# A decoder layer's down projection: token sums stored by gate and up, operands streamed eight tiles ahead, no GpSimd work

## The chip, the core and the metric

The kernel runs on one core of one Trainium2 chip. The metric is device time in microseconds (us); the median of three runs of the kernel before is 1282.82 us (1282.78 to 1285.71). The engines have short names below: PE is TensorE, DVE is VectorE, ACT is ScalarE, POOL is GpSimd, and SP is SyncE, which issues every DMA of this kernel.

## The reference

The layer normalises its input, projects it, runs differential attention and gated linear attention, projects back, and adds the residual; all of this is unchanged. What the change touches is the feed-forward part, for 1024 tokens, a model width of 1024 and 2816 hidden features:

```python
m = rms_norm(h, ffn_norm_gain[l])
h = h + (jax.nn.silu(m @ w_ffn_gate[l]) * (m @ w_ffn_up[l])) @ w_ffn_down[l]
```

`rms_norm` multiplies each token by one factor, 1/sqrt(mean of squares + eps), and each feature by a gain. Everything is float32.

## The kernel before, in words

**Matrix products.** Tensors lie transposed, features on partitions and tokens along the free dimension. A float32 product is made of three fp32r products: each operand is split into a high half (an ACT copy, L248) and a low half (a DVE subtraction, L249) by `split`, and `mm3` (L256 to L259) issues high x high, high x low and low x high, each 128x128 by 128x512.

**Strassen's scheme.** Gate, up and down each multiply two-by-two block matrices in seven products (Winograd's form) in place of eight. The operands are sums and differences of blocks, and the results are sums of the seven products, some of which are accumulated in the same PSUM banks.

**Gate and up** (L1042 to L1107) run over 11 pairs `pr` of feature blocks, each pair for the gate matrix (m = 0) and the up matrix (m = 1). In a pair, `both` runs the seven products with the operands B11, B21, T1, T2, B22, T3 and T4 of the normalised tokens; `a_operands` makes the weight operands a, b, c, d, e, f and g in order, two matrices each, in a ring of four slots (`uh`, `ul`). The sums among them are made by POOL, and by DVE in pair 0. `result` reads a finished quarter q (two token halves by two feature blocks): for the gate it multiplies by the token factor `rsh` and runs the silu on ACT; for up it multiplies with the gate's result into `ac`. Where an earlier partial result has to be added first, the up side's multiplication is POOL's (L1072; DVE's in pair 0). At the end of a pair one DMA of 1 MB stores `ac` in DRAM. The up side's token factor is put off: it is linear, so it is applied at the end of down, to the projected result.

**Pair 0** also makes the token operands T1 to T4 on ACT and DVE (`b_operands`) and the token factor (`rstd_half`).

**Down** (L1115 to L1257) has seven products too, in the order 1, 2, 7, 6, 5, 3, 4, each over 11 steps j and four PSUM banks k, so 12 matmuls a step. Operand a is a sum of activation blocks, operand b one of weight blocks. `sums` loads a raw tile when it needs one and keeps A for later sums; POOL makes the sums of a, DVE those of b. `cut` splits both in rings of three slots. `multiply` issues a product; what stands in `beside` is issued between its steps: reads of finished banks, the token factor, the residual and the stores. In products 5, 3 and 4 POOL's order is the written one. Down's first operands are loaded while the last pair still runs.

**Order.** Except where `manual_schedule` names an engine, a scheduler orders each engine's instructions by its own model of their times; with it, the named engine follows the text. Each engine executes its instructions in order, and a waiting instruction holds up what is behind it on that engine. That holds for SP's queue of DMAs as well: a DMA whose target or source isn't ready holds up the DMAs behind it.

**Memory.** A tile pool that is closed gives its SBUF to the pools opened after it, and a new tile waits for those whose place it takes. `ntp` holds the split tokens, `fl` T2 to T4 and small tiles, `bp` the tiles `gt` and `ac` in two slots each.

Of the kernel before, what the change touches and what calls it, by code (L numbers as in the profile page):

```python
# [9 lines left out]
F32 = mybir.dt.float32  # L10
# [8 lines left out]
P = 128  # L19
T = 1024  # L20
# [136 lines left out]
def decoder_layer(ctx: ExitStack, tc, xt, vecs, lams, w_proj, w_up, w_gu, w_dn, out):  # L157
# [115 lines left out]
    wctx, actx = ExitStack(), ExitStack()  # L273
    wp = wctx.enter_context(pool("wp"))
# [612 lines left out]
    def rstd_half(hf):  # L887
        ps = psum.tile([P, 512], F32, name=f"hn{hf}", tag="ms")
        nc.tensor.matmul(ps, ones, sums[hf], start=True, stop=True)
        a, u = (fl.tile([P, 512], F32, name=f"{nm}{hf}", tag="u2", bufs=2) for nm in "au")  # L890
# [76 lines left out]
    fl = fctx.enter_context(pool("fl"))  # L967
    act_d = [dram.tile([P, 2, T], F32, name=f"act{pr}") for pr in range(NJ // 2)]
# [37 lines left out]
    def a_operands(pr, m):  # L1006
# [11 lines left out]
        def sub(op, a, b, nm):  # L1018
            r = fl.tile([P, 4, P], F32, name=f"{nm}f{pr}_{m}", tag="sf", bufs=4)
# [22 lines left out]
    for pr in range(NJ // 2):  # L1042
# [8 lines left out]
        ac = bp.tile([P, 2, T], F32, name=f"ac{pr}", tag=f"B{pr % 2}")  # L1051
        quarter = lambda q: ac[:, q // 2, 512 * (q % 2) : 512 * (q % 2) + 512]

        def snap(ps, nm, m):
            r = fl.tile([P, 512], F32, name=f"{nm}{pr}_{m}", tag=nm, bufs=2)
            nc.scalar.copy(r, ps)
            return r

        def result(m, q, ps, add):

            if m == 0:
                rs = rsh[:, 512 * (q % 2) : 512 * (q % 2) + 512]
# [53 lines left out]
    with pool("dw") as dw, pool("de") as de, pool("dl") as dlp:  # L1116
        A = {q: [(de if q == "11" else dlp).tile([P, 512], F32, name=f"A{q}_{j}") for j in range(NB)]
             for q in ("11", "12", "21", "22")}
        B = {q: [dlp.tile([P, 512], F32, name=f"B{q}_{j}") for j in range(NB)] for q in ("12", "22")}

        def load_a(q, j):
            t, jj = int(q[0]) - 1, NB * (int(q[1]) - 1) + j
            nc.sync.dma_start(A[q][j], act_d[jj // 2][:, jj % 2, 512 * t : 512 * t + 512])
            return A[q][j]

        def load_b(q, j):
            dst = B[q][j] if q in B else dw.tile([P, 512], F32, name=f"Bs{q}_{j}", tag="bs", bufs=3)
            nc.sync.dma_start(dst, w_dn[int(q[1]) - 1, NB * (int(q[0]) - 1) + j])
            return dst

        def cut(src, nm, tag):
            h = dw.tile([P, 512], F32R, name=f"{nm}h", tag=f"{tag}h", bufs=3)
            l = dw.tile([P, 512], F32R, name=f"{nm}l", tag=f"{tag}l", bufs=3)
            split(src, h, l)
            return h, l

        def temp(nm, tag):
            return dw.tile([P, 512], F32, name=nm, tag=tag, bufs=2)

        def sums(i, j):  # L1140

            asub, aadd = nc.gpsimd.tensor_sub, nc.gpsimd.tensor_add
            bsub, badd = nc.vector.tensor_sub, nc.vector.tensor_add
            if i == 1:
                return load_a("11", j), load_b("11", j)
            if i == 2:
                return load_a("12", j), load_b("21", j)
            if i == 7:
                a = load_a("21", j)
                asub(a, A["11"][j], a)  # L1150
                b, c = load_b("12", j), load_b("22", j)
                bsub(b, c, b)
                return a, b
            if i == 6:
                a = A["21"][j]
                asub(a, load_a("22", j), a)
                b = B["12"][j]
                badd(b, b, load_b("11", j))
                return a, b
            if i == 5:  # L1160
# [16 lines left out]
        def multiply(i, ps, first, beside=(), then=None):  # L1177
# [3 lines left out]
            ab = []  # L1181
            for j in range(NB):
                a, b = sums(i, j)
                ab.append((cut(a, f"da{i}_{j}", "ca"), cut(b, f"db{i}_{j}", "cb")))
                if then is None or j < NB - 2:
                    for k in range(4):
                        one(i, j, k, ps, first, *ab[j])
# [14 lines left out]
        def load_h(q, k):  # L1202
            hr = dw.tile([P, 512], F32, name=f"hr{q}_{k}", tag="hr", bufs=3)
# [3 lines left out]
        def store(q, k, r):  # L1207
# [4 lines left out]
        def tokens(q):  # L1212
            return rsh[:, 512 * (int(q[0]) - 1) : 512 * (int(q[0]) - 1) + 512]

        def last(q, k, ps, r):

            add_last(q, k, scale_last(q, k, ps), r)

        def scale_last(q, k, ps):
            t = dw.tile([P, 512], F32, name=f"t{q}_{k}", tag="st", bufs=4)  # L1220
            nc.vector.tensor_mul(t, ps, tokens(q))
            return t

        def add_last(q, k, t, r):
            nc.vector.tensor_add(r, r, t)
            store(q, k, r)

        def prepare(q, k, r):

            h = load_h(q, k)  # L1230
            nc.gpsimd.tensor_mul(r, r, tokens(q))
            nc.gpsimd.tensor_add(r, r, h)
# [6 lines left out]
        U = banks("U", ("mm", "ms"))  # L1239
        multiply(1, U, True)  # L1240
        for k in K:
            nc.scalar.copy(p1[k], U[k])
        multiply(2, U, False)
        V = banks("V", ("s", "tr"))
        multiply(7, V, True, [lambda k=k: last("11", k, U[k], load_h("11", k)) for k in K])
        for k in K:
            nc.scalar.copy(p7[k], V[k])
        multiply(6, V, False, [lambda k=k: nc.gpsimd.tensor_sub(p7[k], p1[k], p7[k]) for k in K])
        W = banks("W", ("mm", "ms"))
        with tc.manual_schedule(engines=POOL):  # L1250
            multiply(5, W, True, [lambda k=k: both(k) for k in K] + [lambda k=k: prepare("22", k, c22[k]) for k in K])
            t22 = [scale_last("22", k, W[k]) for k in K]
            multiply(3, W, False, [lambda k=k: add_last("22", k, t22[k], c22[k]) for k in K]
                     + [lambda k=k: prepare("12", k, p7[k]) for k in K])
            multiply(4, V, False, [lambda k=k: last("12", k, W[k], p7[k]) for k in K]
                     + [lambda k=k: prepare("21", k, p1[k]) for k in K],
                     lambda k: last("21", k, V[k], p1[k]))  # L1257
# [53 lines left out]
```

## Time and profile before

| | |
|---|---|
| Runs, us | 1285.71, 1282.78, 1282.82; median 1282.82 |
| Profiled execution, us | 1281.03, with a span of 1279.2 from the first instruction to the last |
| Busy in the span | PE 1215.4 us (95%), DVE 849.6 (66%), ACT 578.9 (45%), POOL 381.5 (30%) |
| Mean granted clock of PE | 0.989 |
| DMA | 109.86 MB, 86 GB/s over the span |

The shares are means over stages that differ: attention, the output projection, pair 0 of gate and up until about 635 us, pairs 1 to 10 until 1027.95, then down. Below, "busy" is the time in which an engine worked on an instruction; matmuls are pipelined, so PE's busy time counts a matmul's whole passage, and the pitch from start to start is the better measure. The granted clock is given as a share of the full 2.4 GHz. A wait is idle time of an engine ahead of an instruction, put down to what came last of the things it waited for. The chain of waits goes back from the last instruction, at each step to what released it.

### The profile page before, as it was taken

How to read it: one execution, taken by the hardware profiler on the slowest of the kernel's cores; microseconds unless marked ns; L12 is line 12 of the kernel's file. 1: busy time of each engine (PE TensorE's matmuls, PEld its weight loads, DVE VectorE, ACT ScalarE, POOL GpSimd, SP SyncE). 2: the span in 40 equal slices, each digit the busy share in tenths (PEclk: the TensorE clock that was granted, in tenths of full speed). 3: DMA queues.
4: the chain of work that ended last, by engine and by line, in shares of the span. 5: the costliest groups of instructions: out<-in, count | busy, mean ns of one | idle time of the engine just before them, and what ended most of it. 6: DMA issues, size and time to landing. Idle time of an engine off the chain costs nothing.

```text
span 1279.2 us, 17033 instructions
## 1 busy us (share of the span) xinstructions
PE 1215.4 (95%) x6068; PEld 1010.8 (79%) x6068; DVE 849.6 (66%) x1722; ACT 578.9 (45%) x1171; POOL 381.5 (30%) x354
## 2 busy tenths in 40 slices
PE   7899998999889999999899999999999999898888
PEld 7789888889788887887688888888888887677666
DVE  6764588754888677539754554444555447978987
ACT  5656353665445575526433333333333434343322
POOL 4501314002340000000133543334434204535690
PEclk9999999999999999999999999999999999999999
DMA  6101010201101712410211222121222299610213
GB/s 207 44 22 58 1 50 17 68 16 51 50 17 59 206 58 84 140 67 25 98 66 38 95 99 99 66 72 61 99 99 79 70 314 324 215 60 18 66 50 107
DMA packets 54487, 109.86 MB, mean 86 GB/s; under 512 B 5617, under 2 KB 25218, under 8 KB 50178
## 3 DMA queue, kind: packets, MB, share of 16 engines
q1 hardware_dynamic: 54402, 108.77, 25.3%
q8 instruction: 48, 0.79, 0.3%
q14 instruction: 37, 0.30, 0.1%
HBM read 85.16 MB, written 23.59 MB: 85 GB/s over the span
## 4 chain that ended last, share of the span: by engine, by line
PE 72%; DVE 16%; issue 3%; ACT 3%; POOL 3%; DMA 3%; SPq 0%; DVEq 0%; POOLq 0%; ACTq 0%
PE X L259 6%; PE X L257 6%; PE X L258 6%; PE pp L257 5%; PE pp L259 5%; PE pp L258 4%; PE s L406 3%; PE Z L258 3%; PE Z L259 3%; PE Z L257 3%; PE po L450 2%; PE po L257 2%; PE po L259 2%; PE po L258 2%; PE pa L645 2%
## 5 line engine op out<-in xcount | busy, mean ns | idle before, releaser
L257 PE MATMUL pp<-wh,nh 128*128 128x384 f32 (+1 forms) x512 | 184.5, 361 | 9.9 <-ACT wh L253 7.0
L259 PE MATMUL pp<-wh,nl 128*128 128x384 f32 (+1 forms) x512 | 176.6, 346 | 0.3 <-DVE nl L249 0.3
L258 PE MATMUL pp<-wl,nh 128*128 128x384 f32 (+1 forms) x512 | 176.5, 345 | 0.4 <-DVE wl L254 0.4
L257 PEld LDWEIGHTS pp<-wh,nh 128*128 128x128 f32 x512 | 97.9, 191 | 19.5 <-ACT wh L253 7.4
L1021 POOL TENSOR_TENSOR S1f<-fr 128x512 f32<-128x512 f32 x20 | 31.7, 1587 | 257.9 <-DMA fr<-in_w_gu 257.9
L259 PEld LDWEIGHTS pp<-wh,nl 128*128 128x128 f32 x512 | 97.1, 190 | 3.2 <-issue 2.4
L258 PEld LDWEIGHTS pp<-wl,nh 128*128 128x128 f32 x512 | 97.7, 191 | 2.5 <-DVE wl L254 1.5
L1072 POOL TENSOR_TENSOR ac<-ac,gt 128x512 f32<-128x512 f32 x30 | 45.7, 1524 | 162.8 <-DVE ac L1071 158.1
L419 ACT ACTIVATE e<-e,nm 128x128 f32<-128x128 f32 (+7 forms) x64 | 49.3, 771 | 32.9 <-DVE nm L411 32.8
L546 POOL TENSOR_TENSOR go<-go,gs 128x1024 f32<-128x1024 f32 x4 | 10.2, 2538 | 142.6 <-ACT gs L545 142.6
L257 PE MATMUL po<-mh,wh 128*128 128x512 f32 x128 | 51.2, 401 | 0.0
L259 PE MATMUL po<-mh,wl 128*128 128x512 f32 x128 | 50.6, 395 | 0.0
L258 PE MATMUL po<-ml,wh 128*128 128x512 f32 x128 | 50.4, 394 | 0.0
L1067 ACT ACTIVATE gt<-gt 128x512 f32<-128x512 f32 x44 | 27.7, 632 | 46.7 <-DVE gt L1066 46.6
L254 DVE SCALAR_TENSOR_TENSOR wl<-wr,vec,wh 128x384 fp32r<-128x384 f32 (+1 forms) x64 | 39.3, 640 | 11.6 <-ACT wh L253 11.5
L621 POOL TENSOR_TENSOR X<-bT 128x64 f32<-128x64 f32 x48 | 18.8, 391 | 86.4 <-ACT bT L590 68.6
L249 DVE TENSOR_TENSOR uel<-S4f,ueh 128x512 fp32r<-128x512 f32 x22 | 18.3, 831 | 37.6 <-ACT ueh L248 37.6
L249 DVE TENSOR_TENSOR ufl<-S3f,ufh 128x512 fp32r<-128x512 f32 x22 | 15.1, 692 | 42.1 <-ACT ufh L248 42.1
L411 DVE CUSTOM_DVE_ANT_0 e<-s,ndist 128x512 f32<-128x512 f32 (+3 forms) x64 | 36.8, 586 | 8.1 <-PE s L406 6.5
L450 PE MATMUL po<-v,wT 128*128 128x128 f32 x288 | 39.9, 284 | 2.0 <-ACT wT L440 2.0
L253 ACT ACTIVATE wh<-wr,vec 128x384 fp32r<-128x384 f32 (+1 forms) x64 | 37.4, 613 | 9.0 <-DMA wr<-in_w_proj 6.3
L1021 POOL TENSOR_TENSOR S4f<-fr,S2f 128x512 f32<-128x512 f32 x20 | 29.3, 1467 | 40.4 <-DVE ucl L249 25.5
(598 smaller groups left out, 3646.5 us busy)
## 6 DMA issues: line engine op xcount, KB each, us to landing
fr<-in_w_gu SPq DMA_DIRECT2D x22, 1024.0 KB, 4.9
wr<-in_w_proj SPq DMA_DIRECT2D x72, 192.0 KB, 2.4
act<-ac SPq DMA_DIRECT2D x11, 1024.0 KB, 3.9
A<-act SPq DMA_DIRECT2D x44, 256.0 KB, 5.2
Bs<-in_w_dn SPq DMA_DIRECT2D x44, 256.0 KB, 3.6
B<-in_w_dn SPq DMA_DIRECT2D x22, 256.0 KB, 5.2
h<-in_xt SPq DMA_DIRECT2D x16, 256.0 KB, 5.0
hd<-h SPq DMA_DIRECT2D x16, 256.0 KB, 2.0
```

Of the source, the lines that this page charges most:

```text
L249: nc.vector.tensor_sub(lo, raw, hi.bitcast(F32))
L253: nc.scalar.activation(hi, src, AF.Copy, scale=gain)
L254: nc.vector.scalar_tensor_tensor(lo, src, gain, hi.bitcast(F32), ALU.mult, ALU.subtract)
L257: nc.tensor.matmul(ps, ah, bh, start=first, stop=False, **k)
L258: nc.tensor.matmul(ps, ah, bl, start=False, stop=False, **k)
L259: nc.tensor.matmul(ps, al, bh, start=False, stop=last, **k)
L406: nc.tensor.matmul(ps[m][:, :n], self.qk["q", hq][a][r, P * iq : P * iq + P], self.qk["k", ch][b][r, :n], start=(j == 0), stop=(j == 2))
L411: nc.vector.tensor_tensor_reduce(e[m][:, 512 * ch : 512 * ch + n], ps[m][:, :n], ndist[:, o : o + n], scale=-slope, scalar=nm[:, m, 0:1] i ...
L419: nc.scalar.activation(e[m][:, :cols], e[m][:, :cols], AF.Exp, bias=nm[:, m, nch - 1 : nch], scale=-1.0, accum_out=l[:, m : m + 1])
L450: nc.tensor.matmul(po[:, 0:P], self.wT[i, g][:, P * k : P * k + P], self.v[g][:, k, :], start=(kb == 0), stop=(kb == i))
L1021: (eng.tensor_sub if op == "-" else eng.tensor_add)(r, a, b)
L1072: (nc.vector if pr == 0 else nc.gpsimd).tensor_mul(quarter(q), quarter(q), gt[:, q, :])
```

## The change

- In gate and up, the gate's silu is multiplied by the token factor once more, so that what is stored is complete and down has no token factor left.
- At each pair's end DVE makes four sums of the pair's quarters (`token_sums`): quarter 1 is overwritten by q0 - q1, and `sm` takes q3 less the new quarter 1, that plus q0, and q2 less the first of them. Seven tiles are stored, in two DMAs (`keep`), where there were four. For this, the two feature blocks of a pair are now the two halves of the inner dimension.
- In the last pair, from T3 on, the compute engines follow the written order: the pair's last products, the splitting of down's steps 0 to 2 between them, then the rest of the results, the sums and the store.
- In down, operand a is loaded ready-made, 77 tiles, 8 steps ahead (`load_step`). All weight tiles are loaded once and kept; DVE makes their sums, in place where it can. Operands are cut 3 steps ahead, in rings of five slots. All compute engines follow the written order, and POOL has nothing to do.
- p1, p7 and c22 are read bank by bank at the end of products 1, 7 and 5 (`then`), the last two steps being ordered by bank for it. The residual is added by DVE.
- Tile pools move: `fl` keeps only T2 to T4 and closes with the tokens, the rest goes to `fq`; a spacer `edge` of 24 elements is added.

```diff
+EDGE = 24
+COMPUTE = {mybir.EngineType.PE, mybir.EngineType.Activation, mybir.EngineType.DVE, mybir.EngineType.Pool}
...
+    fl = ntctx.enter_context(pool("fl"))
+    fq = fctx.enter_context(pool("fq", 1, "right"))
+    act_d = [dram.tile([P, 7, 512], F32, name=f"act{pr}") for pr in range(NJ // 2)]
+    A_OF = {1: 0, 7: 1, 2: 2, 4: 3, 6: 4, 5: 5, 3: 6}
...
+        def read(m, q, ps, add):
+
+            dst = gt[:, q, :] if m == 0 else quarter(q)
+            if add is not None:
+                nc.vector.tensor_add(dst, ps, add)
+            elif m == 0:
+                nc.vector.tensor_mul(dst, ps, tokens(q))
+            else:
+                nc.vector.tensor_mul(dst, gt[:, q, :], ps)
+
+        def rest(m, q, add):
+
+            g = gt[:, q, :]
+            if m == 0:
+                if add is not None:
+                    nc.vector.tensor_mul(g, g, tokens(q))
+                nc.scalar.activation(g, g, AF.Silu)
+                nc.vector.tensor_mul(g, g, tokens(q))
+            elif add is not None:
+                (nc.vector if pr == 0 else nc.gpsimd).tensor_mul(quarter(q), quarter(q), g)
+
         def result(m, q, ps, add):
...
+            read(m, q, ps, add)
+            rest(m, q, add)
+
+        def token_sums(sm, k):
+            if k == 0:
+                nc.vector.tensor_sub(quarter(1), quarter(0), quarter(1))
+                nc.vector.tensor_sub(sm[:, 0, :], quarter(3), quarter(1))
+                nc.vector.tensor_add(sm[:, 1, :], sm[:, 0, :], quarter(0))
             else:
...
+                nc.vector.tensor_sub(sm[:, 2, :], quarter(2), sm[:, 0, :])
+
+        def keep(sm):
+            nc.sync.dma_start(act_d[pr][:, 0:4, :], ac)
+            nc.sync.dma_start(act_d[pr][:, 4:7, :], sm)
...
-        both(X, "T3", False, lambda m: result(m, 3, X[m], p5[m]))
-        both(X, "T4", False, lambda m: result(m, 2, X[m], None))
-        nc.sync.dma_start(act_d[pr], ac)
-    fctx.close()
+        if pr + 1 < NJ // 2:
+            both(X, "T3", False, lambda m: result(m, 3, X[m], p5[m]))
+            both(X, "T4", False, lambda m: result(m, 2, X[m], None))
+            token_sums(sm, 0)
+            token_sums(sm, 1)
+            keep(sm)
+
+    cuts = [[next(ops[m]) for m in range(2)] for _ in range(2)]
+    tail = ExitStack()
+    tail.enter_context(tc.manual_schedule(engines=COMPUTE))
+    for m in range(2):
+        product(X[m], cuts[0][m], bop["T3"], False)
+        read(m, 3, X[m], p5[m])
+    for m in range(2):
+        product(X[m], cuts[1][m], bop["T4"], False)
     ntctx.close()
...
+        ORDER = (1, 2, 7, 6, 5, 3, 4)
+        steps = [(i, j) for i in ORDER for j in range(NB)]
+
+        CUT, LOAD = 3, 8
+        b_left = [("21", j) for j in range(NB)] + [(q, j) for j in range(NB) for q in ("22", "12")]
...
+        def load_step(n):
+
+            if n >= len(steps):
+                return
+            i, j = steps[n]
+            araw[n] = da.tile([P, 512], F32, name=f"A{i}_{j}", tag="ar", bufs=LOAD + 2)
+            nc.sync.dma_start(araw[n], act_d[j][:, A_OF[i], :])
+            if i == 1:
+                load_b("11", j)
+            for _ in range(0 if n < LOAD else 1 + (n % 2 if n > 14 else 0)):
+                if b_left:
+                    load_b(*b_left.pop(0))
...
+        def operand_b(i, j):
+            sub, add = nc.vector.tensor_sub, nc.vector.tensor_add
+            b = {q: B[q][j] for q in B}
             if i == 7:
...
+                sub(b["12"], b["22"], b["12"])
+            elif i == 6:
+                add(b["12"], b["12"], b["11"])
+            elif i in (5, 4):
+                t = dw.tile([P, 512], F32, name=f"T{i}_{j}", tag="sb", bufs=3)
+                sub(t, b["22"] if i == 5 else b["21"], b["12"])
+                return t
+            return b[{1: "11", 2: "21", 7: "12", 6: "12", 3: "22"}[i]]
+
+        def cut_step(n):
+            if n < len(steps):
+                i, j = steps[n]
+                ab[i, j] = cut(araw.pop(n), f"da{i}_{j}", "ca"), cut(operand_b(i, j), f"db{i}_{j}", "cb")
...
             for j in range(NB):
...
+                load_step(n0 + j + LOAD)
+                cut_step(n0 + j + CUT)
...
+        for n in range(LOAD):
+            load_step(n)
+        cut_step(0)
+        cut_step(1)
+        rest(0, 3, p5[0])
+        rest(1, 3, p5[1])
+        read(0, 2, X[0], None)
+        cut_step(2)
+        rest(0, 2, None)
+        token_sums(sm, 0)
+        read(1, 2, X[1], None)
+        token_sums(sm, 1)
+        keep(sm)
+        fctx.close()
...
+        U = banks("U", ("ms", "s"))
+        multiply(1, U, True, then=lambda k: nc.scalar.copy(p1[k], U[k]))
         multiply(2, U, False)
...
+        V = banks("V", ("mm", "tr"))
+        multiply(7, V, True, [lambda k=k: last("11", k, load_h("11", k), U[k]) for k in K],
+                 lambda k: nc.scalar.copy(p7[k], V[k]))
+        multiply(6, V, False, [lambda k=k: nc.vector.tensor_sub(p7[k], p1[k], p7[k]) for k in K])
+        W = banks("W", ("ms", "s"))
+        multiply(5, W, True, [lambda k=k: both(k) for k in K],
+                 lambda k: nc.vector.tensor_add(c22[k], c22[k], W[k]))
+        multiply(3, W, False, [lambda k=k: last("22", k, c22[k], load_h("22", k)) for k in K]
+                 + [lambda k=k: (residual("12", k, p7[k]), residual("21", k, p1[k])) for k in K])
+        multiply(4, V, False, [lambda k=k: last("12", k, p7[k], W[k]) for k in K],
+                 lambda k: last("21", k, p1[k], V[k]))
```

## Rows read from the trace of the kernel before

**Rows 1.** Stretches of gate and up: us, each engine busy (instructions), granted clock, DMA share, GB/s.

```profile
640.00:1027.95 387.95, 387.95 (x1664) 311.64 (x1663) 196.03 (x253) 142.20 (x243) 157.01 (x107) 1.00 0.22 81
...
591.00:640.00 49.00, 43.46 (x173) 32.74 (x172) 42.07 (x69) 25.64 (x46) 4.46 (x4) 0.97 0.18 65
```

**Rows 2.** Stretches of down by product: the second, third, fifth and sixth, and the whole.

```profile
1058.12:1090.77 32.65, 30.54 (x134) 24.62 (x132) 23.68 (x30) 13.08 (x25) 13.48 (x9) 1.00 0.97 336
1090.77:1129.94 39.17, 32.99 (x134) 23.91 (x132) 38.80 (x46) 14.08 (x25) 22.21 (x14) 1.00 0.60 189
...
1161.84:1201.82 39.98, 34.44 (x133) 26.19 (x132) 39.91 (x40) 13.83 (x23) 30.04 (x19) 0.91 0.14 40
1201.82:1239.96 38.14, 33.37 (x132) 25.67 (x133) 34.34 (x28) 12.44 (x21) 32.64 (x21) 0.96 0.19 63
...
1027.95:1274.56 246.61, 224.21 (x925) 175.29 (x923) 202.48 (x231) 89.82 (x156) 115.84 (x72) 0.97 0.43 141
```

**Rows 3.** Down's first product, PE in order of time: start us, duration us, instruction.

```profile
1033.64 0.39 PE L257 MATMUL U<-da_2h,db_2h 128*128 128x512 f32 x1
...
1036.36 0.39 PE L257 MATMUL U<-da_3h,db_3h 128*128 128x512 f32 x1
```

**Rows 4.** Waits of PE in down: who for whom, us, times, longest us.

```profile
PE V L258 <- DVE da_1l L249: 3.4, 3, 2.0
```

**Rows 5.** Down, in order of time: first POOL, then DVE.

```profile
1128.98 6.82 POOL L1248 TENSOR_TENSOR p<-p,p 128x512 f32<-128x512 f32 x4
...
1134.58 1.78 DVE L249 TENSOR_TENSOR db_2l<-B,db_2h 128x512 fp32r<-128x512 f32 x1
1136.28 0.68 DVE L249 TENSOR_TENSOR da_2l<-A,da_2h 128x512 fp32r<-128x512 f32 x1
1136.88 0.68 DVE L249 TENSOR_TENSOR db_3l<-B,db_3h 128x512 fp32r<-128x512 f32 x1
```

**Rows 6.** In order of time: ACT in gate and up, ACT in down, then DVE in down.

```profile
865.56 0.63 ACT L1067 ACTIVATE gt<-gt 128x512 f32<-128x512 f32 x1 [1.23 <-DVE gt L1066]
...
1153.65 0.62 ACT L248 CAST db_10h<-B 128x512 fp32r<-128x512 f32 x1 [1.58 <-PE V L258]
...
1154.31 0.69 DVE L249 TENSOR_TENSOR db_10l<-B,db_10h 128x512 fp32r<-128x512 f32 x1 [1.42 <-ACT db_10h L248]
```

**Rows 7.** DMA issues: line, engine, count, size, median us from issue to landing.

```profile
act<-ac SPq DMA_DIRECT2D x11, 1024.0 KB, 3.9
...
A<-act SPq DMA_DIRECT2D x41, 256.0 KB, 5.2
```

**Rows 8.** DVE at a pair's end, in order of time; idle time before it in brackets.

```profile
863.68 1.84 DVE L1066 TENSOR_TENSOR gt<-gt,ndist 128x512 f32<-128x512 f32 x1
...
872.03 1.35 DVE L249 TENSOR_TENSOR ubl<-fr,ubh 128x512 fp32r<-128x512 f32 x1
874.65 0.69 DVE L249 TENSOR_TENSOR ucl<-S1f,uch 128x512 fp32r<-128x512 f32 x1 [1.26 <-ACT uch L248]
```

**Rows 9.** PE at the same pair's second operand, B21, for both matrices.

```profile
877.23 0.39 PE L259 MATMUL Y<-fh,ubl 128*128 128x512 f32 x1
...
880.02 0.39 PE L259 MATMUL Y<-fh,ubl 128*128 128x512 f32 x1
```

**Rows 10.** Waits of PE in pair 0: the first and the last of five lines.

```profile
PE X L259 <- DVE ugl L249: 2.3, 1, 2.3
...
PE X L257 <- DVE ac L1071: 0.3, 1, 0.3
```

**Rows 11.** DVE in pair 0, in order of time.

```profile
632.14 0.69 DVE L1066 TENSOR_TENSOR gt<-X,ndist 128x512 f32<-128x512 f32 x1 [2.00 <-PE X L259]
634.98 0.69 DVE L1069 TENSOR_TENSOR ac<-gt,X 128x512 f32<-128x512 f32 x1 [2.14 <-PE X L259]
```

**Rows 12.** Chain of waits at the very end: start us, us, what.

```profile
1274.95 0.61 DVE t L1221
...
1275.65 0.69 DVE p L1225
```

More of the change, by code (lines that the diff above doesn't have):

```diff
@@ L273, in decoder_layer @@
     wctx, actx = ExitStack(), ExitStack()
+    ctx.enter_context(pool("edge", 1, "right")).tile([P, EDGE], F32, name="edge")
     wp = wctx.enter_context(pool("wp"))
@@ L889, in rstd_half @@
         nc.tensor.matmul(ps, ones, sums[hf], start=True, stop=True)
-        a, u = (fl.tile([P, 512], F32, name=f"{nm}{hf}", tag="u2", bufs=2) for nm in "au")
+        a, u = (fq.tile([P, 512], F32, name=f"{nm}{hf}", tag="u2", bufs=2) for nm in "au")
         y = rsh[:, 512 * hf : 512 * hf + 512]
@@ L1050, in decoder_layer @@
         gt = bp.tile([P, 4, 512], F32, name=f"gt{pr}", tag=f"B{2 + pr % 2}")
-        ac = bp.tile([P, 2, T], F32, name=f"ac{pr}", tag=f"B{pr % 2}")
-        quarter = lambda q: ac[:, q // 2, 512 * (q % 2) : 512 * (q % 2) + 512]
+        ac = bp.tile([P, 4, 512], F32, name=f"ac{pr}", tag=f"B{pr % 2}")
+        quarter = lambda q: ac[:, q, :]
+        tokens = lambda q: rsh[:, 512 * (q % 2) : 512 * (q % 2) + 512]
+        sm = fq.tile([P, 3, 512], F32, name=f"sm{pr}", tag="sm", bufs=1)
         def snap(ps, nm, m):
-            r = fl.tile([P, 512], F32, name=f"{nm}{pr}_{m}", tag=nm, bufs=2)
+            r = fq.tile([P, 512], F32, name=f"{nm}{pr}_{m}", tag=nm, bufs=2)
@@ L1109, in decoder_layer @@
+    cuts = [[next(ops[m]) for m in range(2)] for _ in range(2)]
[6 more added lines that the diff above has]
+        product(X[m], cuts[1][m], bop["T4"], False)
     ntctx.close()
     NB = NJ // 2
[L1116 to L1124, printed above, removed]
-        def load_b(q, j):
-            dst = B[q][j] if q in B else dw.tile([P, 512], F32, name=f"Bs{q}_{j}", tag="bs", bufs=3)
-            nc.sync.dma_start(dst, w_dn[int(q[1]) - 1, NB * (int(q[0]) - 1) + j])
-            return dst
+    with pool("da") as da, pool("dw") as dw:
+        B = {q: [da.tile([P, 512], F32, name=f"B{q}_{j}") for j in range(NB)]
+             for q in ("11",)}
+        ORDER = (1, 2, 7, 6, 5, 3, 4)
+        steps = [(i, j) for i in ORDER for j in range(NB)]
+        CUT, LOAD = 3, 8
+        b_left = [("21", j) for j in range(NB)] + [(q, j) for j in range(NB) for q in ("22", "12")]
+        araw, ab = {}, {}
+        def load_b(q, j):
+            nc.sync.dma_start(B[q][j], w_dn[int(q[1]) - 1, 2 * j + int(q[0]) - 1])
+        def load_step(n):
[9 more added lines that the diff above has]
+                    load_b(*b_left.pop(0))
@@ L1180, in multiply @@
             beside = list(beside)
-            ab = []
+            n0 = ORDER.index(i) * NB
             for j in range(NB):
-                a, b = sums(i, j)
-                ab.append((cut(a, f"da{i}_{j}", "ca"), cut(b, f"db{i}_{j}", "cb")))
+                load_step(n0 + j + LOAD)
+                cut_step(n0 + j + CUT)
                 if then is None or j < NB - 2:
                     for k in range(4):
-                        one(i, j, k, ps, first, *ab[j])
+                        one(i, j, k, ps, first)
                 if j > 0 and beside:
@@ L1193, in multiply, with one @@
                     for j in range(NB - 2, NB):
-                        one(i, j, k, ps, first, *ab[j])
+                        one(i, j, k, ps, first)
                     then(k)
-        def one(i, j, k, ps, first, a, b):
+        def one(i, j, k, ps, first):
+            a, b = ab[i, j]
             sl = slice(P * k, P * k + P)
@@ L1202, in load_h, with last, residual @@
         def load_h(q, k):
-            hr = dw.tile([P, 512], F32, name=f"hr{q}_{k}", tag="hr", bufs=3)
+            hr = dw.tile([P, 512], F32, name=f"hr{q}_{k}", tag="hr", bufs=4)
             nc.sync.dma_start(hr, h_d[int(q[0]) - 1][4 * (int(q[1]) - 1) + k])
             return hr
-        def store(q, k, r):
+        def last(q, k, r, x):
+            nc.vector.tensor_add(r, r, x)
             hf, c = int(q[0]) - 1, 4 * (int(q[1]) - 1) + k
             nc.sync.dma_start(out[P * c : P * c + P, 512 * hf : 512 * hf + 512], r)
-        p1, p7, c22 = ([dlp.tile([P, 512], F32, name=f"{nm}_{k}") for k in range(4)] for nm in ("p1", "p7", "c22"))
[L1212 to L1232, printed above, removed]
+        def residual(q, k, r):
+            nc.vector.tensor_add(r, r, load_h(q, k))
+        for n in range(LOAD):
[12 more added lines that the diff above has]
+        fctx.close()
+        dlp = tail.enter_context(pool("dl", 1, "right"))
+        B.update({q: [dlp.tile([P, 512], F32, name=f"B{q}_{j}") for j in range(NB)] for q in ("21", "22", "12")})
+        p1, p7, c22 = ([dlp.tile([P, 512], F32, name=f"{nm}_{k}") for k in range(4)] for nm in ("p1", "p7", "c22"))
         def both(k):
@@ L1238, in decoder_layer @@
         K = range(4)
[L1239 to L1242, printed above, removed]
+        U = banks("U", ("ms", "s"))
+        multiply(1, U, True, then=lambda k: nc.scalar.copy(p1[k], U[k]))
         multiply(2, U, False)
[L1244 to L1257, printed above, removed]
+        V = banks("V", ("mm", "tr"))
[9 more added lines that the diff above has]
+                 lambda k: last("21", k, p1[k], V[k]))
+        tail.close()
 def _layout(inputs):
```

51 lines of the change are left out of this document (3 added, 48 removed).

## The prediction

> **What bounds the kernel now.** The page's busy shares are means over stages, so I cut the span into stretches by stage first. In gate and up from 640 us on, TensorE (PE) is busy for all of 387.95 us; in pair 0 (591 to 640) for 43.46 of 49 [rows 1]. Down runs from its first matmul, 1027.95, to the end of its last, 1274.56: 246.61 us [rows 2]. One step of it (12 matmuls of 128x512) takes 2.72 us where nothing holds it, 1033.64 to 1036.36 [rows 3]. 77 steps are 77 x 2.72 = 209.4 us, so down loses 37.2 us. Next, its seven products, each 11 steps or 29.9 us: the second stretch loses 2.7 us, the third 9.2, the fifth 10.1, the sixth 8.2, the other three 7.0 together [rows 2]. In the three worst, VectorE (DVE) is busy for 38.80 of 39.17, 39.91 of 39.98 and 34.34 of 38.14 us, and GpSimd (POOL) for 22.21, 30.04 and 32.64 us [rows 2]. The list of waits names what PE lacks: low halves (`split`, L249), which DVE makes [rows 4].
>
> Why DVE is late shows in single instructions in order of time. Beside four POOL instructions (1128.98 to 1135.80) the subtraction L249 takes 1.78 us, after them 0.68, and back to back DVE starts one each 0.60 us [rows 5]. POOL makes A's token sums and the residuals of down.
>
> **Down without POOL.** All POOL work of down goes (44 sums, 4 differences of p7, 24 in `prepare`), and the token factor too (16 multiplications on DVE, 12 of those 24). What DVE keeps, at 0.60 us:
> - two low halves a step, 154; weight sums of products 7, 6, 5 and 4, 44;
> - beside them 4 sums for C11, 4 p7 differences (new on DVE), 8 in `both`, 4 additions to c22 (new), 4 + 8 for C22 and the residuals, 4 for C12, 4 for C21: 40.
>
> 238 x 0.60 = 143 us under 209 us of PE, so the mean is no limit; the order may be, for all four compute engines now follow the written one. In a step with a weight sum DVE makes low half a (0.60) and the sum (0.68 to its end), ScalarE (ACT) copies b's high half (0.62), DVE makes low half b (0.60). The next engine starts 0.04 us after the one before, DVE to ACT (863.68 + 1.84, then 865.56 [rows 6, 8]) as ACT to DVE (1153.65 + 0.62, then 1154.31 [rows 6]). The cycle is 0.60 + 0.68 + 0.04 + 0.62 + 0.04 + 0.60 = 2.58 us, 0.14 under PE's 2.72. One `beside` instruction adds 0.60, so such a step loses 0.46, one with two loses 1.06. Operands are cut 3 steps ahead, 8.2 us. After product 7, ACT's queue has the four copies of V ahead of the next cut; that cut is ready some 3.6 us into product 6, 4.6 us early. Then product 6 loses 4 x 0.46 and gains 7 x 0.14, product 5 loses 4 x 1.06: 4.6 - 1.8 + 1.0 - 4.2 = -0.4. I take +1.0 us (bounds 0, and 20 as in the third rival).
>
> At product ends p1, p7 and c22 are now read bank by bank while the last two steps run. The next product comes to bank 3 nine matmuls (2.0 us) after the end, and the read takes 0.7: no wait. Product 1 uses banks of pair 9 and of Y, read long before.
>
> **DMA.** Down loads 77 A tiles for 44, and 44 weight tiles for 66: 121 against 110 of 256 KB. In its first three steps three tiles a step are 0.79 MB in 2.72 us, 289 GB/s, later 193 to 241; the second stretch moved 336 GB/s [rows 2]. Loads go out 8 steps (21.8 us) ahead and an A tile lands in 5.2 us [rows 7]. This lead also takes away the second stretch's loss, in which DVE's sums stand on weights. Cost 0.
>
> **Into down.** Let E be the end of the last T4 product; a product of 12 matmuls takes 2.80 us here [rows 9]. DVE reads the first X at E - 8.2 and the second at E - 5.4, and by 0.60 us each has made four low halves by E - 2.4: steps 0 and 1 are ready. Then come g's two multiplications round a silu, POOL's product for quarter 3, two low halves beside it, the sums and the last read. I count DVE through at about E + 6.0 and step 3's low halves out at E + 7.2; PE wants them at E + 8.2. The store takes 3.9 us for its first 1 MB [rows 7]. Behind it SP holds the first weight tile that goes where the stored tile lies, and so A tiles 9 and 10, due at E + 24. I take 0; 8 us is the upper bound, if the store takes twice as long as it does now and so do the loads after it.
>
> **Gate and up, pairs 1 to 9.** DVE gets 8 instructions a pair, four token factors behind the silu and four sums, all with both inputs in SBUF; SP one more store of 768 KB. Two factors come in the middle of a pair. Six instructions fall at its end, where DVE is hardly idle until 873.4, and where a multiplication took 1.84 us beside POOL [rows 8]. Behind them stand the low halves of B21's operand, now made by 872.03 + 1.35 = 873.4, which PE first reads at 880.02 [rows 8, 9]: 6.6 us of room. Six cost 3.6 us at 0.60 and 11.0 at 1.84, so a pair pays between 0 and 4.4 us. I expect some 6 us, and DVE's free time from then on (1.26 us ahead of the next instruction [rows 8]) takes up the lag: 0. A gain is excluded, since PE has no idle time there to give back.
>
> The Trainium skill (SBUF — State Buffer, section Who interferes with whom) says that a VectorE instruction with two SBUF inputs and a GpSimd instruction that reads SBUF block each other until one is done. Rows 5 agree, 0.68 against 1.78 us. By that rule the change takes such instructions out of a stage that it frees of POOL and puts others into one that keeps its POOL work; were each of the six to wait, the sum would be the second rival's.
>
> **Pair 0.** POOL does nothing here, DVE runs nearly without a gap from 591 to 630, and PE waits five times, 5.6 us in all, the longest 2.3 us [rows 10]. Of the eight added, three factors come ahead of the g low half that PE waits 2.3 us for, and one sum ahead of a later a half; the others fall into DVE's waits of 2.00 and 2.14 us for X [rows 11]. 4 x 0.60 = +2.4 us (0 if all are put behind, 8 x 0.60 = 4.8 if all lie on the path).
>
> **End.** Behind the last matmul stands one addition to the bank, where a multiplication and an addition stood, 0.70 us from start to start [rows 12]: with the gap, -0.8 us (0 to -1.4).
>
> **Sum.** -37.2 + 1.0 + 0 + 0 + 0 + 2.4 - 0.8 = -34.6 us. The profiled execution took 1281.03 us (span 1279.2 and 1.8 around it): 1246.4. The median of the runs is 1.8 above that execution: 1282.82 - 34.6 = 1248.2.
>
> **Rivals.**
> 1. Down starves once at its start, on the loads behind the store: 8 us, 1256. For it: SP takes its queue in order. Against: A tile 9 has some 12 us of room. Chance 0.05.
> 2. The pair's end gets in PE's way. Mild, 1 to 2 us in each of nine pairs: 1257 to 1266; chance 0.09. Whole, all six at 1.84 us, or the sums standing on DVE for POOL's product of quarter 3 with the low halves queued behind: 4.4 x 9 = 39.6 us, 1288, slower than before. It decides from 34.6 / 9 = 3.8 us a pair. For it: the tight stretch and the 1.84. Against: 6.6 us of room, and half of DVE's time free (196.03 us busy of 387.95 [rows 1]). Chance 0.06.
> 3. Down isn't freed: in written order DVE and ACT wait for each other. If both hand-overs cost 0.3 us more than rows 6 show, a step with a weight sum takes 3.18 us, 0.46 over PE's: 44 x 0.46 = 20 us, 1268. For it: nothing can be moved past a waiting instruction any more. Against: those rows. Chance 0.08.
> 4. The forecast, 1248, own range 1243 to 1254. Chance 0.72.
>
> The range 1243 to 1264 leaves out rival 3, the whole form of 2 and the worst of its mild one. A difference under 0.3% (3.8 us) can't be told from none. Faster 0.93, within 0.3% 0.01, slower 0.06.
>
> **What would show it.** Right: stretches of down near 29.9 us each, granted clock 1.00, L249 at 0.6 to 0.7 us throughout; no PE wait from pair 1 to the end; PE waits of some 8 us in pair 0. Wrong: PE waiting for `ub` low halves at each pair's beginning (2), for `db` low halves in products 7, 6 and 5 (3), or for an A tile in product 1 (1).

## The result and the profile after

| | before | after |
|---|---|---|
| Runs on one chip, us | median 1283.39 (1282.78 to 1285.71, 4 runs) | median 1249.75 (1246.84 to 1253.99, 4 runs) |
| Ratio, 95% interval | | 0.9737 [0.9706, 0.9769] |
| Profiled execution (span), us | 1281.03 (1279.2) | 1249.03 (1247.3) |
| Busy: PE, DVE, ACT, POOL, us | 1215.4, 849.6, 578.9, 381.5 | 1202.8, 877.3, 574.1, 277.0 |
| DMA, MB | 109.86 | 121.41 |

The change made the kernel faster by 33.6 us. I forecast 1248.2, 1.6 us less than the median. The account below goes from the first matmul of one stage to that of the next, in the two profiled executions:

| stage | before | after | difference | forecast |
|---|---|---|---|---|
| up to pair 0 | 586.64 | 587.22 | +0.6 | - |
| pair 0 | 48.07 | 51.24 | +3.2 | +2.4 |
| pairs 1 to 10 | 393.24 | 391.80 | -1.4 | 0 |
| down | 246.61 | 213.17 | -33.4 | -36.2 |
| after the last matmul | 4.64 | 3.87 | -0.8 | -0.8 |
| span | 1279.2 | 1247.3 | -31.9 | -34.6 |

The first line is scatter: over the runs below, gate and up begin between 585.5 and 590.4 us.

Stretches of the kernel after answer to [rows 1, 2]: pair 0, pairs 1 to 10, then the third, fifth and sixth product of down and the whole of it. Columns as in [rows 1].

```profile
587.22:638.46 51.24, 44.76 (x173) 33.89 (x172) 48.93 (x80) 28.32 (x50) 1.30 (x1) 0.93 0.14 51
638.46:1030.26 391.80, 390.68 (x1681) 316.42 (x1680) 272.67 (x331) 139.24 (x244) 169.75 (x109) 1.00 0.30 113
...
1090.12:1120.04 29.92, 29.92 (x133) 24.77 (x132) 22.11 (x35) 12.70 (x24) 0.00 (x0) 1.00 0.56 166
1149.96:1183.54 33.58, 31.65 (x133) 24.31 (x132) 26.91 (x44) 13.68 (x25) 0.00 (x0) 1.00 0.32 94
1183.54:1213.51 29.97, 29.97 (x133) 24.78 (x132) 25.38 (x42) 12.76 (x23) 0.00 (x0) 1.00 0.59 192
1030.26:1243.43 213.17, 211.24 (x925) 172.77 (x923) 151.32 (x240) 89.40 (x158) 1.09 (x1) 1.00 0.50 164
```

The third product took 39.17 us before and is at PE's pitch now (11 x 2.72 = 29.92). DVE is busy in it for 22.11 us against 38.80, and POOL not at all. Five others are at that pitch too. Only product 5, the fifth, takes 33.58.

The granted clock of down is 1.00 where it was 0.97. Before, it fell to half in three stretches, each at or shortly behind a wait of PE of 2.0 to 2.8 us. The longest of them, in the kernel before:

```profile
1179.87:1185.58 5.71, 5.71 (x13) 4.45 (x14) 5.68 (x5) 1.14 (x2) 5.00 (x4) 0.50 0.17 46
```

At 0.50 the matmuls start 0.43 us apart in place of 0.23. PE worked at that level for 12.9 us of down, so by estimate some 6 of the 37.2 us that down lost were not waits but slow matmuls behind them. They went with the waits.

All waits of PE from 560 us to the end, which answer to [rows 4, 10]:

```profile
PE X L262 <- DVE ugl L252: 4.1, 1, 4.1
PE X L262 <- DVE ufl L252: 1.5, 1, 1.5
PE W L260 <- ACT db_10h L251: 1.3, 1, 1.3
PE X L262 <- DVE ual L252: 1.1, 1, 1.1
PE W L260 <- ACT db_8h L251: 0.5, 1, 0.5
PE X L260 <- ACT u L1068: 0.5, 1, 0.5
PE X L260 <- DVE ac L1075: 0.3, 1, 0.3
```

The two on `db` are product 5's. Of the other five, four are pair 0's; the one on `ual` ends at 643.00, in pair 1's first product. The kernel before waits 1.0 us for the same operand there, and [rows 10] counted it with pair 0. From then on PE waits for nothing until product 5.

DVE at the end of a pair, in order of time, answers to [rows 8]; under it is PE at the low halves of B21's operand, as in [rows 9]:

```profile
871.81 1.77 DVE L1099 TENSOR_TENSOR sm<-ac 128x512 f32<-128x512 f32 x1 [1.41 <-POOL ac L1090]
873.50 1.78 DVE L252 TENSOR_TENSOR ual<-fr,uah 128x512 fp32r<-128x512 f32 x1
875.21 1.78 DVE L1100 TENSOR_TENSOR sm<-sm,ac 128x512 f32<-128x512 f32 x1
...
877.51 0.68 DVE L252 TENSOR_TENSOR ubl<-fr,ubh 128x512 fp32r<-128x512 f32 x1
...
879.69 0.68 DVE L252 TENSOR_TENSOR ubl<-fr,ubh 128x512 fp32r<-128x512 f32 x1
...
880.13 0.40 PE L262 MATMUL Y<-fh,ubl 128*128 128x512 f32 x1
...
882.92 0.39 PE L262 MATMUL Y<-fh,ubl 128*128 128x512 f32 x1
```

DVE stands 1.41 us for POOL's product of quarter 3, then three instructions last some 1.78 us beside POOL, whose sums of the next operands run just then:

```profile
871.73 1.30 POOL L1031 TENSOR_TENSOR S1f<-fr 128x512 f32<-128x512 f32 x1
872.99 3.45 POOL L1031 TENSOR_TENSOR S2f<-S1f,fr 128x512 f32<-128x512 f32 x2
```

The low halves come out at 878.19 (gate) and 880.37 (up), 1.9 and 2.6 us ahead of PE. Before, up's had 6.6 us of room [rows 8, 9], and gate's 6.8 (870.41 to 877.23):

```profile
869.23 1.18 DVE L249 TENSOR_TENSOR ubl<-fr,ubh 128x512 fp32r<-128x512 f32 x1
```

So 4.9 and 4.1 us of the room are used up.

The last matmul and DVE behind it answer to [rows 12]:

```profile
1243.20 0.39 PE L262 MATMUL V<-da_10h,db_10l 128*128 128x512 f32 x1
...
1243.63 0.69 DVE L1250 TENSOR_TENSOR p<-p,V 128x512 f32<-128x512 f32 x1 [0.67 <-PE V L262]
```

### The profile page after: what moved, and what is told of

Same layout as the page of the kernel before. It is cut to its first block, busy times and chain, and to the rows that moved or that the text cites. A ratio compares the mean times of both kernels' runs of the same rounds, so it can differ in the third digit from the quotient of the medians.

```text
span 1247.3 us, 17116 instructions
## 1 busy us (share of the span) xinstructions
PE 1202.8 (96%) x6068; PEld 1011.2 (81%) x6068; DVE 877.3 (70%) x1810; ACT 574.1 (46%) x1171; POOL 277.0 (22%) x282
## 2 busy tenths in 40 slices
DMA packets 57656, 121.41 MB, mean 97 GB/s; under 512 B 5969, under 2 KB 25570, under 8 KB 53346
## 4 chain that ended last, share of the span: by engine, by line
PE 81%; DVE 11%; ACT 3%; DMA 2%; issue 2%; POOL 1%; SPq 0%; DVEq 0%; ACTq 0%; POOLq 0%
PE X L262 6%; PE X L261 6%; PE X L260 6%; PE pp L260 5%; PE pp L262 5%; PE pp L261 5%; PE s L411 3%; PE Z L260 3%; PE Z L261 3%; PE Z L262 3%; PE V L260 2%; PE V L262 2%; PE V L261 2%; PE po L455 2%; PE po L260 2%; PE po L262 2%
## 5 line engine op out<-in xcount | busy, mean ns | idle before, releaser
L1031 POOL TENSOR_TENSOR S1f<-fr 128x512 f32<-128x512 f32 x20 | 26.0, 1300 | 254.6 <-DVE gt L1077 245.6
L257 DVE SCALAR_TENSOR_TENSOR wl<-wr,vec,wh 128x384 fp32r<-128x384 f32 (+1 forms) x64 | 39.6, 644 | 12.6 <-ACT wh L256 12.4
L1088 DVE TENSOR_TENSOR gt<-gt,ndist 128x512 f32<-128x512 f32 x44 | 33.5, 762 | 16.4 <-ACT gt L1087 14.7
L252 DVE TENSOR_TENSOR ufl<-S3f,ufh 128x512 fp32r<-128x512 f32 x22 | 15.1, 691 | 41.6 <-ACT ufh L251 41.6
L1031 POOL TENSOR_TENSOR S4f<-fr,S2f 128x512 f32<-128x512 f32 x20 | 33.1, 1657 | 50.1 <-DVE ucl L252 49.4
L650 PE MATMUL pa<-Q,X 128*128 128x128 f32 x224 | 32.4, 292 | 9.3 <-POOL X L637 9.2
```

Source lines behind the costliest of these rows:

```text
L257: nc.vector.scalar_tensor_tensor(lo, src, gain, hi.bitcast(F32), ALU.mult, ALU.subtract)
L1088: nc.vector.tensor_mul(g, g, tokens(q))
```

## The experiments

My theory was the prediction's: in down DVE's instructions last 1.78 in place of 0.68 us while POOL works, and PE starves for low halves. The rival: the sums ready made, the longer lead and the written order are what pays.

**POOL taken off, nothing else (e1).** The kernel before, with POOL's instructions of down given to DVE:

```diff
-            asub, aadd = nc.gpsimd.tensor_sub, nc.gpsimd.tensor_add
+            asub, aadd = nc.vector.tensor_sub, nc.vector.tensor_add
...
-multiply(6, ..., [lambda k=k: nc.gpsimd.tensor_sub(p7[k], p1[k], p7[k]) for k in K])
+multiply(6, ..., [lambda k=k: nc.vector.tensor_sub(p7[k], p1[k], p7[k]) for k in K])
...
-            nc.gpsimd.tensor_mul(r, r, tokens(q))
-            nc.gpsimd.tensor_add(r, r, h)
+            nc.vector.tensor_mul(r, r, tokens(q))
+            nc.vector.tensor_add(r, r, h)
```

> The kernel before, with all of down's POOL work (sums of A, p7 difference, residuals with the token factor) put on DVE and nothing else changed. If POOL holding DVE up is the cause (my theory): DVE has 303 instructions of 0.60 us in down, 182 us under PE's 209, none takes 1.7 us any more, and down falls from 246.6 us to 215 to 225 (some loss stays where two or more instructions stand beside the four of a step, and where weights come late in product 2): 1252 to 1263 us. If the stored sums and the streaming are what pays, and DVE simply has too much to do (rival): 72 more instructions make it later still, 1283 or more.

Measured: 1254.33 us (1252.47 to 1257.22), ratio 0.9776 [0.9757, 0.9796]. Down as a whole:

```profile
1033.78:1247.86 214.08, 212.41 (x925) 172.28 (x923) 185.01 (x303) 90.25 (x156) 0.00 (x0) 1.00 0.50 163
```

DVE gets 72 instructions more (303 against 231) and is busy for less time than before, 185.01 against 202.48 us. This edit alone brings 28.8 us, and down to 214.08. What the rest of the change adds shows in the profiles: 0.9 us in down, 2.0 at the end (e1 needs 5.9 us after the last matmul), and 1.8 lost in pair 0. It nearly cancels, and e1's interval overlaps with the one of the whole change. The 1.8 are uncertain, for the same instructions of pair 0 took 49.49 us in e1 and 48.07 before.

**POOL put back beside the new order (e2).** The kernel after, with one subtraction on POOL in each of the 77 steps, which nobody reads:

```diff
+                x = dw.tile([P, 512], F32, name=f"px{n}", tag="px", bufs=1)
+                nc.gpsimd.tensor_sub(x, ab[i, j][0][0].bitcast(F32), ab[i, j][1][0].bitcast(F32))
```

> The changed kernel, with one POOL subtraction a step in down that nobody needs (two high halves of the step into a spare tile), 77 in all. If a POOL instruction holds up a DVE one for some 1.1 us: a step with a weight sum goes from 2.64 us on DVE to 3.7, 1.0 over PE's 2.72, 44 of them: down 30 to 50 us longer, 1280 to 1300 us, L252 at 1.7 us in down. If down's gain came from the stored sums, the order and the loads alone (rival): 1250 as now.

Measured: 1302.92 us (1301.58 to 1307.05), ratio 1.0158 [1.0137, 1.0179]: slower than before, and a little more than I had expected. Down takes 266.12, 53 us more. DVE and then POOL in it, in order of time:

```profile
1130.70 0.69 DVE L252 TENSOR_TENSOR db_0l<-B,db_0h 128x512 fp32r<-128x512 f32 x1 [0.74 <-ACT db_0h L251]
1131.31 1.78 DVE L252 TENSOR_TENSOR da_1l<-A,da_1h 128x512 fp32r<-128x512 f32 x1
1133.01 0.68 DVE L1202 TENSOR_TENSOR B<-B,B 128x512 f32<-128x512 f32 x1
...
1130.81 1.73 POOL L1214 TENSOR_TENSOR px<-da_0h,db_0h 128x512 f32<-128x512 f32 x1 [2.00 <-ACT db_0h L251]
```

One POOL instruction of 1.73 us stretches the one DVE instruction beside it by 1.1 us, though the two share no data. In down DVE is busy for 213.22 us against 151.32, the granted clock falls to 0.94: 77 such instructions more than undo the whole change. The rule of the Trainium skill that I weighed (SBUF — State Buffer, section Who interferes with whom) agrees with these rows.

**Why product 5 loses 3.7 us (e3, e11).** In the kernel after `cut_step` puts DVE's low half of a ahead of the weight sum, so ACT's copy of b comes behind that sum, and DVE waits for it with nothing else to do. DVE, then ACT, in two steps of product 5:

```profile
1157.74 0.69 DVE L252 TENSOR_TENSOR db_4l<-T,db_4h 128x512 fp32r<-128x512 f32 x1 [0.74 <-ACT db_4h L251]
1158.35 0.68 DVE L1276 TENSOR_TENSOR c<-V,p 128x512 f32<-128x512 f32 x1
1158.95 0.68 DVE L1277 TENSOR_TENSOR p<-V,p 128x512 f32<-128x512 f32 x1
1159.55 0.68 DVE L252 TENSOR_TENSOR da_5l<-A,da_5h 128x512 fp32r<-128x512 f32 x1
1160.15 0.68 DVE L1205 TENSOR_TENSOR T<-B,B 128x512 f32<-128x512 f32 x1
1161.57 0.69 DVE L252 TENSOR_TENSOR db_5l<-T,db_5h 128x512 fp32r<-128x512 f32 x1 [0.74 <-ACT db_5h L251]
...
1160.92 0.62 ACT L251 CAST db_5h<-T 128x512 fp32r<-128x512 f32 x1 [2.69 <-DVE T L1205]
```

1161.57 - 1157.74 = 3.83 us for such a step, against PE's 2.72. e3 has the sum made first, so that DVE cuts a while ACT copies b:

```diff
-                ab[i, j] = cut(araw.pop(n), f"da{i}_{j}", "ca"), cut(operand_b(i, j), f"db{i}_{j}", "cb")
+                b = operand_b(i, j)
+                ab[i, j] = cut(araw.pop(n), f"da{i}_{j}", "ca"), cut(b, f"db{i}_{j}", "cb")
```

> The changed kernel, with the weight sum of a step ahead of the low half of a, so that ACT copies b's high half while DVE makes a's low half. If product 5 loses its 3.7 us because DVE waits 0.74 us in each step for ACT and so never gains on PE (my theory): DVE's cycle falls from 2.64 to about 2.0 us, no PE wait is left in down, product 5 takes 29.9 us, 1246 us. If it is the two readings of V beside each step that are too much for any order (rival): product 5 stays at 33.6 us, 1250.

Measured: 1247.98 us (1245.67 to 1251.88), ratio 0.9731 [0.9709, 0.9752]. The fifth product and down as a whole:

```profile
1151.24:1181.16 29.92, 29.92 (x133) 24.77 (x132) 23.39 (x38) 12.32 (x21) 0.00 (x0) 1.00 0.36 97
1031.52:1241.01 209.49, 209.49 (x925) 173.23 (x923) 151.36 (x240) 90.20 (x158) 1.10 (x1) 1.00 0.52 167
```

Down is at PE's pitch, 77 x 2.72. The wait was the cause. This is the fastest version; it ran once more beside the kernel after, on one chip:

> The changed kernel, nothing altered, beside the next one on one chip. If the change is what the runs so far show, 1250 us (1247 to 1254), product 5 of down 33.6 us and the other six 29.92. Two theories on the pitch of the gate and up pairs (39.04 us in its first profile, 39.20 in others): set by where the operands lie, then 39.04 again in every pair; not set by the program, then 39.20 in some or all pairs.

> The changed kernel with the other factor of a down step made ahead of its cut, once more, beside the changed kernel. If product 5's 3.7 us are lost by VectorE's wait for ScalarE in each step, down is 209.5 us against 213.2 and the time 3 to 4 us under the run beside it. If the pitch of the pairs is not set by the program, the pairs can be at 39.04 or 39.20 here, up to 1.8 us in the time, which could hide half of it.

Measured: the kernel after 1252.28 us (1251.73 to 1252.69), ratio 0.9753 [0.9738, 0.9768]; e3 1247.43 (1246.02 to 1251.47), ratio 0.9725 [0.9705, 0.9744]. Product 5 took 33.59 and 29.93, down 213.16 and 209.47, as in the first runs. The medians differ by 4.9 us; the two intervals overlap a little.

I suspected that the order of the last two steps had a share too. By it step 10's operands are used nine matmuls earlier, and the longest wait of down, 1.3 us, is for them. e11 has only the last step ordered by bank in product 5:

```diff
-                if then is None or j < NB - 2:
+                tail = 1 if i == 5 else 2
+                if then is None or j < NB - tail:
...
-                    for j in range(NB - 2, NB):
+                    for j in range(NB - tail, NB):
```

> The changed kernel with product 5's second last step in plain order (all four banks of step 9, then step 10 bank by bank), so that step 10's operands are first used 2.04 us (nine matmuls) later than now. In the changed kernel the lead of step 10's low half over its first matmul is used up by steps of 3.83 us on VectorE and by this order. If the order has a 2.0-us share in the 3.7 us that product 5 loses, it takes 31.6 us here (31.4 to 32.0), product 3 stays at 29.9 to 30.3, and the time is 1248 against 1250. If the loss is the slow steps' alone and step 10 would have been late anyhow, product 5 stays at 33.0 to 33.6.

Measured: 1252.19 us (1251.53 to 1253.7), ratio 0.9747 [0.9716, 0.9778]; product 5 takes 33.45. The wait for step 10 is gone, and another stands behind the product. PE, then DVE:

```profile
1186.32 0.47 PE L260 MATMUL W<-da_0h,db_0h 128*128 128x512 f32 x1 [1.54 <-DVE c L1290]
...
1181.27 0.69 DVE L252 TENSOR_TENSOR db_10l<-T,db_10h 128x512 fp32r<-128x512 f32 x1 [0.74 <-ACT db_10h L251]
...
1185.49 2.48 DVE L1290 TENSOR_TENSOR c<-c,W 128x512 f32<-128x512 f32 x4
```

The additions that read product 5's banks stand on DVE behind six low halves, and the next product needs the banks. I had the mechanism wrong: DVE itself is late, and whatever PE needs of it next is late by as much.

**Pair 0 (e5).** e3's edit, and pair 0's factors behind the silu, its up multiplications, sums and store collected and issued in pair 1 behind T1:

```diff
-                nc.vector.tensor_mul(g, g, tokens(q))
+                if pr == 0:
+                    late.append(lambda g=g, t=tokens(q): nc.vector.tensor_mul(g, g, t))
+                else:
+                    nc.vector.tensor_mul(g, g, tokens(q))
...
+        if pr == 1:
+            put_off()
         both(X, "T2", False, snap2)
```

> The changed kernel with the weight sum ahead of a's low half (as in e3), and with pair 0's token factors behind the silu, its up multiplications, its four sums and its store put off into pair 1, behind T1 there. If the 3.2 us that pair 0 grew by are DVE instructions ahead of the g low half on DVE's queue (my theory): the wait for `ugl` falls from 4.1 us to under 1, pair 0 takes some 47 us for 51.2, and pairs 1 on stay at 39.04; with e3's 3.7 us about 1243. If pair 1 has no room for what is put off, or the wait is for something else (rival): pair 1 grows by what pair 0 loses, 1246 to 1248.

Measured: 1248.2 us (1246.52 to 1249.18), ratio 0.9735 [0.9712, 0.9758], no better than e3. The scheduler, which orders gate and up, started the collected instructions earlier than the text has them, from 631.78 us on, behind `ugl` and before pair 0 ends. The wait for `ugl` falls from 4.1 to 1.1 us and pair 0 from 50.81 in e3 to 46.38. But pair 1 takes 43.91 against 40.90: there three of the collected instructions stand beside POOL, at 1.77 to 1.80 us each, and half clock, which stood in pair 0 in e3, now falls into pair 1 (0.50 from 638.67 to 641.40). Pair 2 takes 39.79 against 39.04. Of 4.4 us 0.7 are left.

**Room at the pairs' ends (e7), and the first cuts (e6).** e7 has four more subtractions on DVE between the pair's sums; e6 has steps 0 to 2 of down cut behind the last pair's sums and stores:

```diff
             token_sums(sm, 0)
+            for k in range(4):
+                nc.vector.tensor_sub(sm[:, 2, :], quarter(k), quarter(0))
             token_sums(sm, 1)
```

```diff
-        cut_step(0)
-        cut_step(1)
         rest(0, 3, p5[0])
...
-        cut_step(2)
...
         keep(sm)
+        for n in range(CUT):
+            cut_step(n)
```

> The changed kernel with four more subtractions of quarters at each pair's end, which nobody needs. In the changed kernel B21's low halves are ready 2.0 us (gate) and 2.6 us (up) ahead of PE. Four more cost DVE 2.4 us at 0.60 and 6.8 at 1.7: PE waits 0.4 to 4.8 us at the start of nine pairs, 4 to 43 us in all, 1262 as the middle. This is the second rival of the prediction, pushed past its point. If the room is larger than these rows show because DVE's idle time takes it up (the prediction's reason to expect 0): 1250.

> The changed kernel with the operands of down's first three steps split behind the last pair's results and store instead of between its last products. If the place of these splits is what lets PE run on into down (my working: DVE is through at 6.0 us after the last product, then one step per 1.2 us): PE stands about 6 to 7 us at the start of down, steps 1 and 2 follow without a further wait, 1256. If DVE or ACT have the room anyway (rival): 1250.

Measured: e7 1259.31 us (1254.61 to 1260.78), ratio 0.9817 [0.9787, 0.9847]; pairs 3 to 9 take 39.6 to 40.0 in place of 39.04, and pair 1 44.07 against 40.44, with a wait of 3.0 us for `ual`. The time is near what I had expected, the place is not. In pair 3, DVE and then PE:

```profile
755.42 1.83 DVE L1144 TENSOR_TENSOR sm<-ac 128x512 f32<-128x512 f32 x1
757.17 0.68 DVE L1075 TENSOR_TENSOR gt<-X,p 128x512 f32<-128x512 f32 x1
...
758.00 0.47 PE L260 MATMUL X<-T4h,ugh 128*128 128x512 f32 x1 [0.61 <-DVE gt L1075]
```

One of the added subtractions (L1144), stretched beside POOL, stands ahead of DVE's read of the bank X, which the product with T4 needs; it does so in six of these seven pairs. The low halves of B21 still come out 2.0 and 2.8 us ahead of PE, so their room wasn't touched.

e6 1257.24 us (1253.49 to 1259.59), ratio 0.9801 [0.9768, 0.9835]; down's first product takes 34.97 us, 5.0 more, of which 3.2 are one wait for `da_0l`; behind it the granted clock is at half until 1041.0. The split inside the last pair is worth 5 us; I had expected 6 to 7.

**The pairs' pitch (e4, e8).** Pairs 2 to 10 took 39.20 us each before and 39.04 after, all nine alike, which no step of mine explains. The theory: the spacer, by which the operands lie elsewhere.

```diff
-    ctx.enter_context(pool("edge", 1, "right")).tile([P, EDGE], F32, name="edge")
```

```diff
-EDGE = 24
+EDGE = 88
```

> The changed kernel without the spacer tile, so that the tiles of the right side of SBUF move by 96 bytes. If the place of the stationary operand sets the shorter pitch of gate and up (5.575 us a product of 24 matmuls for 5.600 before): products of 5.600 us again, 77 x 0.025 = 1.9 us, about 1251.6. If the spacer does nothing and the pitch comes from something else (rival): 5.575 and 1249.7.

> The changed kernel with a spacer of 88 elements instead of 24, so that the right side's tiles lie another 256 bytes lower; the stationary operands of gate and up then begin 128 bytes past a multiple of 512, as those of down do, whose pitch is 226.7 ns for 232.4. If the place within 512 bytes sets the pitch: 5.44 us a product, 10 us less, 1240. If only whether a tile begins at a multiple of 64 bytes counts (e4 against the changed kernel): 5.575 as now, 1250.

Measured: e4 1252.47 us (1250.76 to 1256.03), ratio 0.9763 [0.9744, 0.9783], with pairs at 39.20, as the theory has it. e8 1249.42 (1248.12 to 1250.64), ratio 0.9746 [0.9722, 0.977]: pairs 2 to 4 take 39.04 and pairs 6 to 10 take 39.20, in one run. e6, whose spacer is the kernel after's, has 39.20 throughout; e3 has 39.04 throughout, and the same program a second time (e10) changes in the middle. Starts of its pairs, PE:

```profile
795.91 0.39 PE L260 MATMUL X<-fh,uah 128*128 128x512 f32 x1
...
834.95 0.39 PE L260 MATMUL X<-fh,uah 128*128 128x512 f32 x1
...
874.15 0.39 PE L260 MATMUL X<-fh,uah 128*128 128x512 f32 x1
```

834.95 - 795.91 = 39.04, 874.15 - 834.95 = 39.20. The theory falls: one program shows both. The 1.4 us can't be credited to the change, and their cause is open.

## Why the prediction was right, point by point

- **Down without POOL: right.** L252 lasts 0.68 to 0.69 us in down, but for one of 1.42 beside the last pair's POOL product, and e1 and e2 show from both sides that POOL's presence was the loss.
- **Product 5, +1.0 forecast, +3.7 measured: the term that was mis-sized.** The step read 4.6 - 1.8 + 1.0 - 4.2 = -0.4 us of lead. From the trace of after, the time from the end of a step's low half b to its first matmul (at step 4 of product 5: 1160.84 - 1158.43 = 2.41) was 3.83 us at step 3 of product 6 (I had 4.6), 1.84 after the four p7 differences (-2.0), and 2.41 ahead of the reads of product 5 (+0.6, since the cycle is 1147.19 - 1144.55 = 2.64 us and not 2.58). Four steps of 3.83 us take 4.4, which by reckoning leaves -2.0; in the trace it stops at -0.7, since PE waits meanwhile. Four small errors of one sign make 1.6 us. The rest is the product's end, which I had counted as costing nothing: e11 shows that it costs some 1.8 us in either order, as long as DVE is late. That an idle gap of 0.74 us in each step could be closed by exchanging two lines, I didn't see.
- **Pair 0, +2.4 forecast, +3.2 measured.** DVE in order of time, as in [rows 11]:

```profile
620.65 1.28 DVE L1088 TENSOR_TENSOR gt<-gt,ndist 128x512 f32<-128x512 f32 x2
...
626.33 0.68 DVE L1088 TENSOR_TENSOR gt<-gt,ndist 128x512 f32<-128x512 f32 x1
...
630.54 0.68 DVE L252 TENSOR_TENSOR ugl<-fr,ugh 128x512 fp32r<-128x512 f32 x1
```

  PE's five waits of [rows 10] come to 7.5 us (I had some 8). Three factors ahead of `ugl`, as forecast, are 1.8 us, and PE's wait for it grows from 2.3 to 4.1. Most of the remaining 1.4 us is the granted clock, for which the sum had no term. Behind that wait PE works at half clock, before and after:

```profile
629.77:632.76 2.99, 2.99 (x9) 2.31 (x8) 0.99 (x2) 0.00 (x0) 0.00 (x0) 0.50 0.89 342
...
631.28:636.56 5.28, 5.28 (x12) 4.12 (x13) 3.75 (x6) 0.24 (x1) 0.00 (x0) 0.50 0.78 265
```

  Some 2 us more at 0.43 us from matmul to matmul in place of 0.23 cost 0.9 by estimate; shorter waits at g's first matmuls make up the rest.
- **Pairs 1 to 9, 0: right, with less to spare than it sounds.** I expected 6 us of lag in 6.6 of room; 4.1 to 4.9 were used. In its second profile the kernel after lost 1.0 us in pair 2 and 0.5 in pair 5, with waits of 0.9 us in all that the profile puts down to `uah`. Like those of e7 in pairs 3 to 9 they stand at the first matmul with T4, at a pair's end. The waits for B21's low halves, rival 2's sign, appear in no run. Four instructions more cost 0.6 to 1.0 us a pair there, but not where I had looked for it.
- **Into down and DMA, 0: right.** The first product takes 29.94 us; its waits are none. DVE is through with the last pair at 6.3 us behind T4's end (I had 6.0).
- **End, -0.8: right.**
- **The other rivals.** PE never waits for an A tile (1); steps with one weight sum take DVE 2.64 us, 0.06 over my count and still under PE's pitch, for the hand-overs cost 0.09 us to ACT and 0.03 back (step 5 of product 5 above; I had 0.04 each), not 0.3 more; rival 3's sign, PE's waits for `db`, shows in product 5 alone, where two reads come on top (3).
- **The sum: closer than its terms.** In the profiles down gained 2.8 us less than forecast and pair 0 lost 0.8 more, and 1.4 us of the pairs' pitch, which the change can't be credited with, made up a part. That the median lies 1.6 us from the forecast is in part luck.

The prediction did not price the spacer, which is part of the change; e4 and e8 show no price that follows it.

## What to carry to other kernels

Where VectorE is late, first look whether its own instructions are stretched by GpSimd beside them: moving GpSimd's work onto the engine that looked full made that engine less busy. Then keep an account, step by step, of how far the late engine is ahead of TensorE, for a cycle a little under TensorE's pitch gives back almost nothing of what longer steps take (here 0.08 us a step against 1.1). Order each step so that the other engine's hand-over lies beside work, not behind it.

## What the runs showed of the hardware that was not expected

Matmuls of one shape and at a granted clock of 1.00 follow each other by 226.7 ns in down (2.72 us / 12) in every run, and by 232.4 or 233.3 ns in gate and up (39.04 or 39.20 us / 168). The latter two alternate between executions of one program and within one, with no wait of PE in the list.
